# Loading x in tiles of 128 tokens instead of 116, and sending the norm factors of the dt path through DRAM

## The chip, the cores and the metric

One core of one Trainium2 chip runs the whole program. TensorE (PE) multiplies matrices and also turns them (a product with the identity); its weight loads are listed apart as PEld. VectorE (DVE), ScalarE (ACT) and GpSimd (POOL) work on tiles in on-chip memory, each through its own instructions in a fixed order; SyncE (SP) and ScalarE issue transfers, which run on 16 DMA engines. The metric is the device time of the core in microseconds, as the median of several runs: 3075.25 us before the change (3 runs, 3072.14 to 3075.53).

## The reference

A hybrid decoder trunk: 16 learned meta tokens are put ahead of 1024 tokens of width 1024, then come a Mamba-2 (SSD) mixer, a gated feed-forward layer with a short convolution, stick-breaking attention with shared keys and values, and a second feed-forward layer. The change touches only the very start:

```python
h = jnp.concatenate([meta_tokens, x], axis=1)            # 1040 tokens
u = _rmsnorm(h, ssd_norm)                                # x * rsqrt(mean(x*x) + eps) * gain
z, xbc, dt_raw = jnp.split(u @ w_in, [...], axis=-1)     # the last 32 columns are dt_raw
dt = jax.nn.softplus(dt_raw + dt_bias)
...                                                      # conv, SSD scan, gate, h + ... @ w_out
```

So the start needs x turned (features on the partitions, tokens along the row), its norm factor for each token, the normalized and turned x as the operand u of all projections, and dt_raw for the path that makes the decays of the SSD scan.

## The kernel before

**Tokens.** The 1040 tokens are cut into nine chunks of 116 (the last has 112), `CH`, and into three groups of three chunks, `TT`: 348, 348 and 344 tokens. The projections work on one group at a time, so a projection of one block of 128 output columns is three tiles. The SSD scan works on chunks of 116 and the dt path puts chunk i of group j at column `[i, j]` of a tile with 116 partitions.

**`load_x`.** Nine tiles hold x, one chunk each, tokens on the partitions; the pool has `XB` = 8 buffers, so the ninth tile waits until the first is no longer read. The loads go alternately to SyncE's and ScalarE's queue (L296 to L299). `stream(j)` takes a group: three squares with a sum over the row, on VectorE for the chunks in `SQD` (L318) and else on ScalarE (L320); then for each of eight blocks k of 128 features three transposes into a PSUM bank of the pool `lg` (two buffers, L325), a copy of it to the tile h (ScalarE for odd k, L328, VectorE for even k, L330) and a matmul that adds block k to dt_raw (L331); then the norm factors of the group from the sums (`token_rstd`, L204 to L210), written to `r9`. With the third group each finished h row is stored to DRAM (`h_d`, L333), from where the mixer's residual fetches it much later. `scaled(j)` multiplies the three x tiles in place by their factors (L342), turns them again, block by block, into PSUM banks of the pool `sm` (L347), and `parts` (L258 on ScalarE, L259 on VectorE) splits each with the gain into a high and a low part, uh and ul. `ORD` sets the order of these six pieces in the text: stream 0, scaled 0, stream 1, scaled 1, stream 2, scaled 2; products of u with the weights (`mm3`, L153 to L155, three per block) come as soon as their operands are there.

**Weights.** `load_w` fetches 128 x 1024 floats by SyncE's queue (L139) into one of three buffers, which the tile wdt of dt's weights shares; ScalarE rounds them to the high part (L146) and GpSimd subtracts (L147).

**dt path.** Its first steps turn the dt rows (L398), multiply them by the factors `r9` (L407, VectorE) and add a bias; the path is a generator, advanced between the first projections, and its result goes to DRAM (acs_d, ea_d) and back, as the decays of the scan.

**Order.** Up to the scan the instructions are ordered by the framework: each engine's list is fixed at build time, by when the framework's own model expects operands and buffers to be ready. On each engine it is then worked off strictly in order. Transfers that one queue issues wait in its order as well.

Of the kernel before, what the change touches and what calls it, by code (L numbers as in the profile page):

```python
# [20 lines left out]
CB = 116  # L21
CH = [(c * CB, min(CB, L - c * CB)) for c in range(9)]
TT = [(0, 348), (348, 348), (696, 344)]
# [24 lines left out]
SUMS = ((6, 1), (3, 6), (7, 6), (3, 5), (5, 7)), ((4, 7), (2, 1))  # L48
LPOOL = ((2, 2), (2, 4), (2, 6), (2, 7))
ORD = ((0, 0), (1, 0), (0, 1), (1, 1), (0, 2), (1, 2))  # L50
XB, SQD = 8, (1, 4, 7)
SCALE = 0.125


# [12 lines left out]
class Trunk:  # L67
# [213 lines left out]
    def load_x(self, pool, mx):  # L281

        nc, a = self.nc, self.a
        H = HEADS
        ss = self.cp.tile([P, 9], F32, tag="ss0", name="ss0")
        nc.vector.memset(ss, 1.0)
        wdt = self.wp.tile([P, 1024], F32, tag="w32", name="wdt")
        self.ln_exp()
        d = self.dp.tile([KD, P, L], F32, tag="h0_d", name="h0_d")
        r9 = mx.tile([P, 3, 3], F32, tag="r9", name="r9")  # L290
        dt = self.ex("dtr")
        xs = []
# [12 lines left out]
        u = [(self.Q("uh", F32R), self.Q("ul", F32R)) for _ in range(KD)]  # L305
        for t in (t for hl in u for t in hl):
            nc.gpsimd.tensor_copy(t[:, :HALO], self.zero)
        hs = [self.Q("h") for _ in range(KD)]

        def stream(j):  # L310
            s0, nn = TT[j]
            x3 = xs[3 * j : 3 * j + 3]
            for i in range(3):
                c = 3 * j + i
                n = CH[c][1]
                t = self.wp.tile([P, D], F32, tag="wl", name=self.nm("junk"))
                if c in SQD:
                    nc.vector.scalar_tensor_tensor(t[:n, :], x3[i][:n, :], 1.0, x3[i][:n, :], op0=ALU.mult, op1=ALU.mult, accum_out=ss[:n, c : c + 1])  # L318
                else:
                    nc.scalar.activation(t[:n, :], x3[i][:n, :], AF.Square, accum_out=ss[:n, c : c + 1])  # L320
            for k in range(KD):
                ps = self.lg("xT")
                for i in range(3):
                    n = CH[3 * j + i][1]
                    nc.tensor.transpose(ps[:, i * CB : i * CB + n], x3[i][:n, k * P : k * P + P], self.ident[:n, :n])  # L325
                h = hs[k][:, s0 : s0 + nn]
                if k % 2:
                    nc.scalar.activation(h, ps[:, :nn], AF.Copy)  # L328
                else:
                    nc.vector.tensor_copy(h, ps[:, :nn])  # L330
                nc.tensor.matmul(dt[j * H : j * H + H, :nn], wdt[:, k * H : k * H + H], h, start=k == 0, stop=k == KD - 1)  # L331
                if j == 2:
                    nc.sync.dma_start(d[k], hs[k][:, :L])  # L333
            self.token_rstd(ss[:, 3 * j : 3 * j + 3], CB, 3, y=r9[:, :, j])

        def scaled(j):
            s0, nn = TT[j]
            x3 = xs[3 * j : 3 * j + 3]
            for i, t in enumerate(x3):
                n = CH[3 * j + i][1]  # L340
                r = r9[:n, i : i + 1, j]
                nc.vector.tensor_scalar(t[:n, :], t[:n, :], r, None, op0=ALU.mult)  # L342
            for k in range(KD):
                ps = self.sm("xr")
                for i in range(3):
                    n = CH[3 * j + i][1]
                    nc.tensor.transpose(ps[:, i * CB : i * CB + n], x3[i][:n, k * P : k * P + P], self.ident[:n, :n])  # L347
                self.parts(ps[:, :nn], u[k], s0, nn, self.par("ssd_norm", k))
# [1183 lines left out]
```

## Time and profile before

| | |
|---|---|
| median of 3 runs | 3075.25 us (3072.14 to 3075.53) |
| the profiled execution, span | 3077.5 us |
| busy: PE, DVE, ACT, POOL | 94%, 76%, 53%, 46% |
| bytes read from and written to HBM | 201.25 MB, 53.45 MB |
| loads of x | 400 KB (with 64 KB of meta), seven of 464 KB, 448 KB |
| other loads at the start | params 272 KB, wdt 128 KB, heads 32 KB, weights 512 KB each |
| first dt transposes (L398) | at 102.2 us |

The profile shows one execution, 2.25 us above the median of the runs. A row of the timeline or of the chain begins with the start and the length in us; "out<-in" names the tiles by the program's names without their numbers; what stands in brackets is how long the engine had been idle before and what released it. In a row by stretches stand the stretch, its length, then for each engine its busy time with the number of instructions, and last the clock that TensorE was granted (1.00 is full), the busy share of the 16 DMA engines and the GB/s that they moved.

### The profile page before, as it was taken

Reading aid. Unit: us, or ns where it says so; the run is one execution under the profiler, and the core shown is the slowest. Engines: PE = TensorE matmul, PEld = TensorE weight load, DVE = VectorE, ACT = ScalarE, POOL = GpSimd, SP = SyncE. Lnnn points to the kernel's source line nnn. Section 1 sums busy time; section 2 is a strip of 40 time slices with the busy share of each in tenths; the row PEclk is TensorE's granted clock in tenths of the full one; section 3 lists DMA queues with packets and bytes.
Section 4 is the critical chain, followed back from the end, with each engine's and each line's share of the span. In section 5 each row is a group of like instructions: output and inputs, shape, how many; then the busy total and the mean of one; then the engine's idle time right before and its main releaser. Section 6 shows DMA issues by size and latency. Waiting matters only on the chain.

```text
span 3077.5 us, 58674 instructions
## 1 busy us (share of the span) xinstructions
PE 2897.7 (94%) x22535; PEld 2782.2 (90%) x22535; DVE 2336.0 (76%) x4030; ACT 1645.5 (53%) x3403; POOL 1411.6 (46%) x1289
## 2 busy tenths in 40 slices
PE   5999999989998999998999999999897999998997
PEld 2999898879988999998999999999797999998996
DVE  3576868885369888778966888888759888888874
ACT  2555545553245555654334888777635555554332
POOL 1154435452335666657733222222225666666741
PEclk8999999999999999999999999999998999999998
DMA  3333323323221222244132222221431222225221
GB/s 110 108 93 93 105 88 109 101 71 138 70 83 56 83 77 75 80 136 152 47 122 77 64 60 67 62 57 48 140 112 59 80 84 77 76 86 179 76 97 55
DMA packets 123220, 273.41 MB, mean 89 GB/s; under 512 B 13468, under 2 KB 53020, under 8 KB 122940
## 3 DMA queue, kind: packets, MB, share of 16 engines
q1 hardware_dynamic: 117622, 258.54, 26.9%
q10 hardware_dynamic: 4054, 6.56, 0.6%
q8 instruction: 177, 2.90, 0.4%
q0 software_dynamic: 1264, 4.57, 0.4%
q14 instruction: 103, 0.84, 0.1%
HBM read 201.25 MB, written 53.45 MB: 83 GB/s over the span
## 4 chain that ended last, share of the span: by engine, by line
PE 67%; DVE 17%; ACT 5%; issue 5%; DMA 3%; POOL 2%; ACTq 0%; POOLq 0%; SPq 0%; DVEq 0%
PE p L153 9%; PE p L154 9%; PE p L155 9%; PE acc L153 5%; PE acc L154 5%; PE acc L155 5%; PE pj L153 5%; PE pj L154 5%; PE pj L155 5%; DVE gl L992 3%; PE po L1297 2%; PE lg L1255 2%; DMA x<-in_x 1%; PE wT L1282 1%; DVE D L573 1%
## 5 line engine op out<-in xcount | busy, mean ns | idle before, releaser
L153 PE MATMUL pj<-uh,wh 128*128 128x348 f32 (+2 forms) x1536 | 507.0, 330 | 16.1 <-DVE qs L1206 7.2
L154 PE MATMUL pj<-ul,wh 128*128 128x348 f32 (+2 forms) x1536 | 497.3, 324 | 0.0
L155 PE MATMUL pj<-uh,wl 128*128 128x348 f32 (+2 forms) x1536 | 495.6, 323 | 0.0
L154 PE MATMUL p<-bl,fh 128*128 128x262 f32 x1408 | 400.9, 285 | 14.1 <-DVE bl L814 14.1
L153 PE MATMUL p<-bh,fh 128*128 128x262 f32 x1408 | 402.1, 286 | 2.5 <-ACT fh L845 1.4
L155 PE MATMUL p<-bh,fl 128*128 128x262 f32 x1408 | 400.1, 285 | 0.0
L846 POOL TENSOR_TENSOR fl<-x,fh 128x1024 fp32r<-128x1024 f32 x88 | 212.5, 2416 | 353.3 <-ACT fh L845 275.4
L147 POOL TENSOR_TENSOR wl<-w,wh 128x1024 fp32r<-128x1024 f32 (+2 forms) x80 | 163.9, 2051 | 351.8 <-ACT wh L146 351.7
L153 PEld LDWEIGHTS pj<-uh,wh 128*128 128x128 f32 x1536 | 291.8, 190 | 23.7 <-DVE qs L1206 9.2
L154 PE MATMUL p<-bl,wh 128*128 128x262 f32 x1056 | 303.1, 287 | 8.7 <-DVE bl L814 8.7
L153 PE MATMUL p<-bh,wh 128*128 128x262 f32 x1056 | 302.3, 287 | 6.2 <-ACT bh L813 6.2
L155 PE MATMUL p<-bh,wl 128*128 128x262 f32 x1056 | 301.2, 286 | 0.0
L154 PEld LDWEIGHTS pj<-ul,wh 128*128 128x128 f32 x1536 | 292.0, 190 | 1.2 <-issue 0.5
L155 PEld LDWEIGHTS pj<-uh,wl 128*128 128x128 f32 x1536 | 291.4, 190 | 0.5 <-issue 0.2
L278 DVE SCALAR_TENSOR_TENSOR c<-p,params,c 128x260 f32<-128x260 f32 x528 | 251.4, 484 | 47.2 <-ACT c L275 37.5
L153 PE MATMUL acc<-gh,wh 128*128 128x260 f32 x896 | 262.1, 293 | 22.9 <-DVE p L1037 10.7
L154 PEld LDWEIGHTS p<-bl,fh 128*128 128x128 f32 x1408 | 267.2, 190 | 16.3 <-DVE bl L814 16.0
L153 PEld LDWEIGHTS p<-bh,fh 128*128 128x128 f32 x1408 | 266.8, 190 | 5.2 <-ACT bh L813 2.0
L154 PE MATMUL acc<-gl,wh 128*128 128x260 f32 x896 | 260.3, 291 | 9.8 <-DVE gl L992 9.5
L155 PEld LDWEIGHTS p<-bh,fl 128*128 128x128 f32 x1408 | 266.6, 190 | 0.1
L886 DVE TENSOR_TENSOR c<-c,c 128x260 f32<-128x260 f32 x176 | 255.7, 1453 | 7.5 <-ACT c L882 4.5
L155 PE MATMUL acc<-gh,wl 128*128 128x260 f32 x896 | 259.0, 290 | 1.2 <-POOL wl L990 1.2
(311 smaller groups left out, 8566.7 us busy)
## 6 DMA issues: line engine op xcount, KB each, us to landing
w<-in_w_up SPq DMA_DIRECT2D x88, 512.0 KB
g<-c SPq DMA_DIRECT2D x176, 130.0 KB
w<-in_w_down SPq DMA_DIRECT2D x44, 512.0 KB
w<-in_w_in SPq DMA_DIRECT2D x40, 512.0 KB
b<-g SPq DMA_DIRECT2D x32, 520.0 KB
E<-ea_d SPq DMA_DIRECT2D x32, 464.0 KB
D<-acs_d SPq DMA_DIRECT2D x32, 420.5 KB
h<-h_d SPq DMA_DIRECT2D x16, 520.0 KB
```

The lines of the kernel that those rows point to most:

```text
L147: nc.gpsimd.tensor_tensor(wl[:, :n], w32[:, :n], wh[:, :n].bitcast(F32), op=ALU.subtract)
L153: mm(out, wh, uh, start=first, stop=False, skip_group_check=joins)
L154: mm(out, wh, ul, start=False, stop=False, skip_group_check=joins)
L155: mm(out, wl, uh, start=False, stop=last, skip_group_check=joins)
L278: nc.vector.scalar_tensor_tensor(out, ps[:, o + i : o + i + n], wcol(i), out, op0=ALU.mult, op1=ALU.add)
L573: nc.vector.tensor_scalar(dk[:, i], dk[:, i], self.cols[:n, 1, cc, h0 + i : h0 + i + 1], 0.0, op0=ALU.subtract, op1=ALU.min)
L846: tt(lo[:, :n], t, hi[:, :n].bitcast(F32), op=ALU.subtract)
L886: self.last_up = tt(g[:, :FN], g[:, :FN], v[:, :FN], op=ALU.mult)
L992: tt(gl, x, gh.bitcast(F32), op=SUB)
L1255: nc.tensor.matmul(ps[:nt, :m], part[:, c0 : c0 + nt], ks[a][:, s0 : s0 + m], start=x == 0, stop=x == 1)
L1282: nc.tensor.transpose(pt[:ns, x * CB : x * CB + nt], bt[a][:nt, x * CB : x * CB + ns], self.ident[:nt, :nt])
L1297: nc.tensor.matmul(po[64 * a : 64 * a + 64, w], v[: CH[c][1], c, 64 * a : 64 * a + 64], wt[a][: CH[c][1], c, :nt], start=x == 0, stop=x == ...
```

## The change

x is loaded in nine tiles of 128 tokens, `XC`: the first has 16 meta rows and 112 of x, the last only 16 rows. All nine have a buffer. Three tiles make a group, so the groups in which x is squared, turned, copied and split are 384, 384 and 272 tokens (`XG`). The tiles of the projections and the matmuls of dt keep the old groups of 348, 348 and 344 and the old chunks of 116. Since the factors now lie by tiles of 128 (`rx`) and the dt path wants them by chunks of 116, `rx` is written to DRAM by one transfer (128 partitions x 9 floats, each float to its own place) and read back by three (116 x 3 floats each).

```diff
-XB, SQD = 8, (1, 4, 7)
+XC = [(c * P, min(P, L - c * P)) for c in range(9)]
+XG = [(0, 3 * P), (3 * P, 3 * P), (6 * P, L - 6 * P)]
+XB, SQD = 9, (1, 4, 7)
...
+        rx = mx.tile([P, 9], F32, tag="rx", name="rx")
...
-        for c, (t0, n) in enumerate(CH):
+        for c, (t0, n) in enumerate(XC):
             xt = pool.tile([P, D], F32, tag="x", name=self.nm("x"), bufs=XB)
...
+        def turned(bank, j, k):
+            ps = bank("xT")
+            for i in range(3):
+                n = XC[3 * j + i][1]
+                nc.tensor.transpose(ps[:, i * P : i * P + n], xs[3 * j + i][:n, k * P : k * P + P], self.ident[:n, :n])
+            return ps[:, : XG[j][1]]
+
         def stream(j):
+            g0, gn = XG[j]
             s0, nn = TT[j]
...
             for k in range(KD):
-                ps = self.lg("xT")
-                for i in range(3):
-                    n = CH[3 * j + i][1]
-                    nc.tensor.transpose(ps[:, i * CB : i * CB + n], x3[i][:n, k * P : k * P + P], self.ident[:n, :n])
-                h = hs[k][:, s0 : s0 + nn]
+                ps = turned(self.lg, j, k)
+                h = hs[k][:, g0 : g0 + gn]
...
-                nc.tensor.matmul(dt[j * H : j * H + H, :nn], wdt[:, k * H : k * H + H], h, start=k == 0, stop=k == KD - 1)
+                nc.tensor.matmul(dt[j * H : j * H + H, :nn], wdt[:, k * H : k * H + H], hs[k][:, s0 : s0 + nn], start=k == 0, stop=k == KD - 1)
                 if j == 2:
                     nc.sync.dma_start(d[k], hs[k][:, :L])
-            self.token_rstd(ss[:, 3 * j : 3 * j + 3], CB, 3, y=r9[:, :, j])
+            self.token_rstd(ss[:, 3 * j : 3 * j + 3], P, 3, y=rx[:, 3 * j : 3 * j + 3])

         def scaled(j):
...
+            for c in range(3 * j, 3 * j + 3):
+                n = XC[c][1]
+                nc.vector.tensor_scalar(xs[c][:n, :], xs[c][:n, :], rx[:n, c : c + 1], None, op0=ALU.mult)
             for k in range(KD):
...
+                self.parts(turned(self.sm, j, k), u[k], *XG[j], self.par("ssd_norm", k))

         for step, j in ORD:
             (scaled if step else stream)(j)
+        rd = self.dp.tile([9, P], F32, tag="r_d", name="r_d")
+        nc.sync.dma_start(rd.rearrange("c p -> p c"), rx)
+        flat = rd.rearrange("c p -> (c p)")
+        for j in range(3):
+            nc.sync.dma_start(r9[:CB, :, j], flat[3 * CB * j : 3 * CB * (j + 1)].rearrange("(i p) -> p i", p=CB))
         return d, u, dt, r9
```

The change moves instructions, since the framework orders them anew. Three places, by the lists of the engines (line, operation, out<-in, partitions x elements; numbers tell tiles of one name apart, and x_106, x_111, x_113, ... x_125 are the nine tiles of x before, x_107, x_112, ... x_126 those of now).

ScalarE, the issue of the ninth tile of x. Before, between parts of the first group:

```order
L258 ACTIVATE uh_137<-xr_262,params 128x348
L328 ACTIVATE h_166<-xT_328 128x348
L258 ACTIVATE uh_139<-xr_268,params 128x348
L299 DMA x_125<-in_x 112x1024
L258 ACTIVATE uh_141<-xr_274,params 128x348
L320 ACTIVATE junk_397,ss_99<-x_125 112x1024
```

Now, the first instructions of ScalarE, and further down the squares of group 2:

```order
L300 DMA x_107<-in_x 112x1024
L302 DMA x_114<-in_x 128x1024
L302 DMA x_118<-in_x 128x1024
L302 DMA x_122<-in_x 128x1024
L302 DMA x_126<-in_x 16x1024
L329 ACTIVATE junk_168,ss_99<-x_107 128x1024
...
L329 ACTIVATE junk_285,ss_99<-x_120 128x1024
L334 ACTIVATE h_163<-xT_192 128x384
L207 ACTIVATE rx<-ss_99 128x3
L329 ACTIVATE junk_394,ss_99<-x_122 128x1024
L208 ACTIVATE rx<-rx 128x3
L329 ACTIVATE junk_398,ss_99<-x_126 16x1024
L334 ACTIVATE h_165<-xT_204 128x384
```

The ninth tile is issued with the others, and the squares of x_120, x_122 and x_126 (sixth, seventh and ninth tile) now stand ahead of the copy h_165 of group 0.

SyncE's queue behind the last tile of x that it loads. Before:

```order
L299 DMA x_123<-in_x 116x1024
L139 DMA w_95_518<-in_w_in 128x1024
L139 DMA w_98_524<-in_w_in 128x1024
L333 DMA h_d<-h_159 128x1040
L333 DMA h_d<-h_160 128x1040
L139 DMA w_111_655<-in_w_in 128x1024
L333 DMA h_d<-h_161 128x1040
```

Now:

```order
L302 DMA x_124<-in_x 128x1024
L141 DMA w_95_524<-in_w_in 128x1024
L141 DMA w_98_530<-in_w_in 128x1024
L141 DMA w_111_661<-in_w_in 128x1024
L352 DMA r_d<-rx 128x9x1
L141 DMA w_120_768<-in_w_in 128x1024
L355 DMA r_104<-r_d 116x3x1 x3
L141 DMA w_129_880<-in_w_in 128x1024
L339 DMA h_d<-h_161 128x1040
```

The third, fourth and fifth weight tile stand ahead of all stores of h, and the four transfers of the factors among them; behind the three loads (which wait for the store of the factors) stand one weight tile and the eight stores of h.

VectorE, where the dt path first uses the factors. Before:

```order
L259 SCALAR_TENSOR_TENSOR ul_140<-xr_502,params,uh_139 128x344
L259 SCALAR_TENSOR_TENSOR ul_142<-xr_508,params,uh_141 128x344
L407 TENSOR_TENSOR dt_637<-dt_629,r_104 116x288
L408 TENSOR_TENSOR dt_637<-dt_637,heads 116x288
L278 SCALAR_TENSOR_TENSOR xbc_661<-pj_692,params,xbc_661 128x348 x2
```

Now:

```order
L261 SCALAR_TENSOR_TENSOR ul_141<-xT_503,params,uh_140 128x272
L261 SCALAR_TENSOR_TENSOR ul_143<-xT_509,params,uh_142 128x272
L411 TENSOR_TENSOR dt_643<-dt_635,r_104 116x288
L412 TENSOR_TENSOR dt_643<-dt_643,heads 116x288
L280 SCALAR_TENSOR_TENSOR xbc_667<-pj_698,params,xbc_667 128x348 x2
```

The place is the same: right behind the last parts of group 2, ahead of the convolution taps (L278, now L280) that read a projection's bank.

More of the change, by code (lines that the diff above doesn't have):

```diff
@@ L308, in load_x @@
         hs = [self.Q("h") for _ in range(KD)]
+        def turned(bank, j, k):
[4 more added lines that the diff above has]
+            return ps[:, : XG[j][1]]
         def stream(j):
+            g0, gn = XG[j]
             s0, nn = TT[j]
-            x3 = xs[3 * j : 3 * j + 3]
-            for i in range(3):
-                c = 3 * j + i
-                n = CH[c][1]
+            for c in range(3 * j, 3 * j + 3):
+                n = XC[c][1]
@@ L316, in stream @@
                 t = self.wp.tile([P, D], F32, tag="wl", name=self.nm("junk"))
                 if c in SQD:
-                    nc.vector.scalar_tensor_tensor(t[:n, :], x3[i][:n, :], 1.0, x3[i][:n, :], op0=ALU.mult, op1=ALU.mult, accum_out=ss[:n, c : c + 1])
+                    nc.vector.scalar_tensor_tensor(t[:n, :], xs[c][:n, :], 1.0, xs[c][:n, :], op0=ALU.mult, op1=ALU.mult, accum_out=ss[:n, c : c + 1])
                 else:
-                    nc.scalar.activation(t[:n, :], x3[i][:n, :], AF.Square, accum_out=ss[:n, c : c + 1])
+                    nc.scalar.activation(t[:n, :], xs[c][:n, :], AF.Square, accum_out=ss[:n, c : c + 1])
@@ L321, in stream @@
             for k in range(KD):
-                ps = self.lg("xT")
-                for i in range(3):
-                    n = CH[3 * j + i][1]
-                    nc.tensor.transpose(ps[:, i * CB : i * CB + n], x3[i][:n, k * P : k * P + P], self.ident[:n, :n])
-                h = hs[k][:, s0 : s0 + nn]
+                ps = turned(self.lg, j, k)
+                h = hs[k][:, g0 : g0 + gn]
                 if k % 2:
-                    nc.scalar.activation(h, ps[:, :nn], AF.Copy)
+                    nc.scalar.activation(h, ps, AF.Copy)
@@ L329, in stream @@
                 else:
-                    nc.vector.tensor_copy(h, ps[:, :nn])
-                nc.tensor.matmul(dt[j * H : j * H + H, :nn], wdt[:, k * H : k * H + H], h, start=k == 0, stop=k == KD - 1)
+                    nc.vector.tensor_copy(h, ps)
+                nc.tensor.matmul(dt[j * H : j * H + H, :nn], wdt[:, k * H : k * H + H], hs[k][:, s0 : s0 + nn], start=k == 0, stop=k == KD - 1)
                 if j == 2:
                     nc.sync.dma_start(d[k], hs[k][:, :L])
-            self.token_rstd(ss[:, 3 * j : 3 * j + 3], CB, 3, y=r9[:, :, j])
+            self.token_rstd(ss[:, 3 * j : 3 * j + 3], P, 3, y=rx[:, 3 * j : 3 * j + 3])
@@ L336, in scaled @@
         def scaled(j):
[L337 to L342, printed above, removed]
-            for k in range(KD):
[L344 to L348, printed above, removed]
+            for c in range(3 * j, 3 * j + 3):
+                n = XC[c][1]
+                nc.vector.tensor_scalar(xs[c][:n, :], xs[c][:n, :], rx[:n, c : c + 1], None, op0=ALU.mult)
```

## The prediction

> **What bounds the kernel now.** I read the page first, to see what the program as a whole waits for, then the chain of waits over the first 70 us, where every line of the change lies, and then the busy times by stretch.
>
> ```profile
> span 3077.5 us, 58674 instructions
> PE 2897.7 (94%) x22535; PEld 2782.2 (90%) x22535; DVE 2336.0 (76%) x4030; ACT 1645.5 (53%) x3403; POOL 1411.6 (46%) x1289
> PE   5999999989998999998999999999897999998997
> ```
>
> TensorE is busy for 94% of the span, and of its 40 slices (77 us each) the first is by far the emptiest. Work that arrives sooner there pulls everything behind it forward, as long as TensorE stays the bound behind it. The chain of waits says what the first slice waits for (start us, us, what):
>
> ```profile
> 6.43 35.52 DMA x<-in_x
> 41.98 1.23 DVE junk L318 x2
> ...
> 44.18 6.18 DVE x L342 x3
> 50.40 0.84 PE xr L347 x3
> ...
> 54.28 0.77 PE xT L325 x3
> ...
> 55.37 1.18 PE dtr L331 x2
> ...
> 57.47 0.70 PE dtr L331 x2
> 58.17 0.45 PE xT L325 x3
> ...
> 64.05 3.43 DMA x<-in_x
> ```
>
> Up to 41.98 us it is the load of x and nothing else, then the scaling of the first three tiles (L342), then TensorE, whose dt matmuls and transposes take 1.18 and 0.77 here and 0.70 and 0.45 a little later, at half and at full clock; at 64.05 the ninth tile is fetched, which had no buffer before, and TensorE waits again. By stretch (us from:to, length, busy time and count of PE, PEld, DVE, ACT, POOL, granted clock, DMA share, GB/s):
>
> ```profile
> 6.50:42.00 35.50, 10.88 (x28) 3.63 (x28) 4.58 (x14) 7.50 (x17) 0.61 (x1) 0.77 0.35 119
> 42.00:50.40 8.40, 5.17 (x25) 2.39 (x24) 8.33 (x11) 2.81 (x4) 5.41 (x2) 0.91 0.04 17
> 50.40:64.50 14.10, 14.10 (x61) 6.79 (x61) 7.47 (x14) 4.76 (x11) 0.00 (x0) 0.79 0.01 2
> 64.50:67.50 3.00, 0.01 (x1) 0.00 (x0) 0.58 (x1) 0.48 (x1) 0.00 (x0) 0.84 0.50 153
> 67.50:102.50 35.00, 34.51 (x192) 26.23 (x193) 17.67 (x38) 20.41 (x38) 2.36 (x1) 0.92 0.51 182
> 102.50:150.00 47.50, 45.88 (x286) 45.16 (x285) 30.46 (x63) 26.65 (x39) 9.91 (x5) 1.00 0.35 89
> 72.00:76.00 4.00, 4.00 (x22) 3.09 (x21) 1.96 (x7) 1.96 (x3) 0.00 (x0) 0.83 0.98 351
> ```
>
> From 50.4 us on TensorE is the bound (14.10 of 14.10, 34.51 of 35.00, 45.88 of 47.50), but for 3.00 us at 64.5. Before that it works 16 us out of 44.
>
> **Why x is slow.** Packets, MB and share of 16 engines by queue, first from 9 to 17 us, where only 116-row tiles move, then from 64.5 to 67.5 (the 112-row tile alone):
>
> ```profile
> q10 hardware_dynamic: 104, 0.41, 12.8%
> q1 hardware_dynamic: 105, 0.41, 12.7%
> ...
> q10 hardware_dynamic: 128, 0.46, 50.1%
> ```
>
> Two queues together use 25.5% of 16 engines: four engines, without a break. A packet takes 0.255 x 16 x 8.0 us / 209 = 156 ns, or 26 GB/s per engine. The 112-row tile needed 0.501 x 16 x 3.0 / 128 = 188 ns a packet and landed 3.43 us after its issue, though its 448 KB are hardly less than the others' 464; from 72 to 76 us, where 128-row tiles of h and w move, the share is 0.98. So a row count of 116 confines a transfer to four engines, and counts of 112 and 128 do not.
>
> **The change, part by part.** *The load.* x is 1040 rows of 4 KB, 4.26 MB, and params, wdt and heads with it are 272, 128 and 32 KB. On 16 engines of 26 GB/s (412 GB/s) that is 11.4 us; at the 351 GB/s that 72 to 76 us showed it is 13.4. The start costs about 2.3 us: 3.43 less seven packets per engine of 156 ns. So x is in at 13.7 to 15.7 us; I take 14.7 for the eighth and ninth tile, 13.2 for the sixth and seventh, against 41.98 and 67.48 now.
>
> *From there to the first scaled transposes.* These rows price the steps (start us, us, engine, line, what; the last is the line's own view, with least, median and greatest ns):
>
> ```profile
> 6.50 1.06 ACT L320 ACTIVATE junk<-x 116x1024 f32<-116x1024 f32 x1 [4.42 <-DMA x<-in_x]
> 7.46 0.19 ACT L320 ACTIVATION_READ_ACCUMULATOR junk<-x 116x1 f32 x1
> 18.34 0.46 ACT L328 ACTIVATE h<-xT 128x348 f32<-128x348 f32 x1 [1.47 <-PE xT L325]
> 39.57 0.20 ACT L205 ACTIVATE r<-ss 116x3 f32<-116x3 f32 x1
> 44.09 6.26 DVE L342 TENSOR_SCALAR x<-x,r 116x1024 f32<-116x1024 f32 x3
> 44.39 5.41 POOL L147 TENSOR_TENSOR wl<-w,wh 128x1024 fp32r<-128x1024 f32 x2 [34.47 <-ACT wh L146]
> ...
> L342 DVE TENSOR_SCALAR x<-x,r x9: 747/751/2849, 44.1 to 87.2; 116x1024 f32<-116x1024 f32 x8, 112x1024 f32<-112x1024 f32 x1
> ```
>
> Today ScalarE and TensorE have long done group 0 when the eighth tile lands. In the new order ScalarE must, from 13.2 us, square the sixth tile (1.25), copy an h (0.46), take a factor (0.20), square the seventh (1.25), a factor (0.20), the ninth (1.25; 16 rows, but the same 1024 elements in each), and only then copy the h of block 5 (0.46): 18.3 us. TensorE follows with a dt matmul (0.70 in the chain) and the last transposes of group 0 (0.45): 19.5. The scaling overwrites tiles that these read, so it starts at about 19.6, and takes 6.2 as now, since GpSimd's two weight splits (5.41) fall on the same time again. It ends at 25.8 against 50.4 now: **-24.6**. If the splits miss it, three scalings of 0.75 (the median of nine) take 2.3 and it is -28.5; if x comes 1 us later and TensorE is still at half clock (0.77 and 1.18), -22.8. With x 1 us early the far end is -29.5.
>
> *The ninth tile* has a ninth buffer and comes with the rest: the idle 3.00 us go, **-3.0**.
>
> *The clock.* In 67.5:102.5 it is 0.92, so 35.0 x 0.08 = 2.8 us of TensorE's work is lost to the dip that the wait at 64.5 leaves; **-2.8**, or 0 if another stall there does the same. In 50.4:64.5 it is 0.79, 14.1 x 0.21 = 3.0 lost after the stall behind the scaling. That stall comes back, at 20 to 26 us, so I leave this at 0 (-3.0 to +3.0).
>
> [...]
>
> *VectorE* was busy 7.47 + 0.58 + 17.67 = 25.7 of the 52.1 us from 50.4 to 102.5, and nothing waited long for it. The same work now has 47 us. What can bunch is the second scaling: if GpSimd's split of the third weight meets it, it takes up to 6.2 in place of 2.3, and TensorE stands behind it. **+1.0** (0 to +4).
>
> *Widths.* 384, 384 and 272 columns sum to the same 1040: the copies, parts and transposes that grow in two groups shrink in the third. 0. From the dt transposes on, the order on TensorE, VectorE and ScalarE is the old one but for a few neighbours swapped, so there is nothing to gain or lose: 0.
>
> *The factors through DRAM.* One store of 1152 single floats, three loads of 348. The nearest packets are the 464-byte ones of acs_d and ea_d, from 129 to 131.5 us, and their user is the first row below of VectorE:
>
> ```profile
> q1 hardware_dynamic: 495, 0.20, 34.6%
> ...
> 102.82 0.46 DVE L407 TENSOR_TENSOR dt<-dt,r 116x288 f32<-116x288 f32 x1 [0.22 <-PE dt L398]
> ```
>
> 0.346 x 16 x 2.5 / 495 = 28 ns each. The third factors are ready at about 27 us, a copy and three small steps behind the scaling in VectorE's order. The store has 72 packets on each of 16 engines (2.0 us), the loads, 116 rows again, 261 on each of four (7.3), with two starts of 2.3: in at about 41. VectorE asks at 102.8 - 29.4 = 73.4. **0**: 32 us of projections and transposes hide it. Behind the loads on SP's queue stand one weight tile (block 4), which TensorE's order wants six projections after the dt transposes, and the eight stores of h: the same cover and more. A packet would have to take (73.4 - 27 - 4.6) / 0.333 = 125 ns, nearly the price of 4 KB, to be seen.
>
> [...]
>
> **Sum.** -24.6 - 3.0 - 2.8 + 1.0 = -29.4. The profiled execution goes from 3077.5 to 3048.1; the median of the runs shown is 2.25 lower, 3075.25, which gives **3046**. With all the near or all the far ends of the terms the gain is 19 to 38.
>
> **Rivals.** *The start is bound by its own engines.* With x in early, half clock and VectorE's bunches set the pace up to the projections. For: in 42.00:50.40 VectorE is busy 8.33 of 8.40, and ScalarE's squares now crowd its copies. Against: from 25.8 on the order has projections to fill with. If 25 us go at half clock, 12.5 are lost in place of 3.0, and with VectorE's +4.0 in place of +1.0 the gain is 29.4 - 9.5 - 3.0 = 16.9: 3058.
>
> *The transfer is no faster.* If four engines still carry 128 rows, only the ninth tile's wait and its clock loss go: 5.8, 3069; with a new stall there, nothing. Against it stands the 0.98 of 72 to 76 us.
>
> *The factors come late, and it is slower.* Place: VectorE at the first use of r9. Behind it in VectorE's order stand the taps that free the projections' banks, so TensorE stops too. It decides from 125 ns a packet, and eats the whole gain at (102.8 - 27 - 4.6) / 0.333 = 214 ns; at 300 ns the factors land at 131.5, 29 us after the place where they are used now: 3104. For: no packet of 4 bytes with data is in this trace. Against: 464 bytes cost 28 ns.
>
> *More gain:* splits that miss the scaling and no first clock dip, over 38 us, below 3037.
>
> **Chances.** Forecast (19 to 38 us) 0.75, bound by its own engines (6 to 19) 0.13, more gain 0.03, transfer no faster 0.05 (of which 0.02 shows a gain), late factors 0.04. The runs shown spread over 3.4 us, so 0.2%, 6 us, is about what can be told from no change. Faster 0.93, within 0.2% 0.03, slower 0.04. The range, 3037 to 3058, holds the forecast and the nearer part of the first rival.
>
> **What would show it.** Right: the eighth tile lands by 16 us with the DMA share above 0.8 from 4 to 14; the scaling of group 0 begins near 20 and ends near 26; the dt transposes stand near 73 in place of 102.4; VectorE's first use of r9 waits for no DMA; behind that the two traces run alike. Wrong: a DMA share near 0.25, a half clock that lasts beyond 35 us, VectorE waited for by TensorE for over 5 us between 26 and 60, or a wait of VectorE for r_d.

## The result

The changed kernel takes **3047.6 us** (median of 4 runs, 3044.1 to 3050.1) against 3074.7 (4 runs, 3072.1 to 3075.5): a ratio of 0.9918, 95% interval 0.9904 to 0.9932, or 27.1 us less. The forecast was 3046, with a range of 3037 to 3058.

The page of the changed kernel, the lines that answer to the first ones shown of before:

```profile
span 3045.5 us, 58682 instructions
PE 2890.8 (95%) x22535; PEld 2779.1 (91%) x22535; DVE 2336.8 (77%) x4030; ACT 1646.9 (54%) x3403; POOL 1414.2 (46%) x1289
PE   8999999989989999999999999999998999998996
```

The first slice of TensorE has gone from 5 to 8 tenths, and the rest looks as before. The chain of waits over the first 70 us (start us, us, what):

```profile
2.18 12.41 DMA x<-in_x
14.61 1.15 ACT junk L329 x2
...
22.05 2.23 DVE ss L206
...
25.13 1.41 DVE x L345 x2
26.54 2.23 DVE tb L209
```

The chain waits for x until 14.6 us instead of 42.0, and the scaling of group 0 (L345) ends at 26.5 instead of 50.4. What arrives at 14.6 is the fourth tile. Later tiles are still under way, as ScalarE's wait for the sixth shows (timeline, ScalarE):

```profile
16.34 1.06 ACT L329 ACTIVATE junk<-x 128x1024 f32<-128x1024 f32 x1 [0.48 <-DMA x<-in_x]
```

By the semaphore events of their loads in the trace, the sixth tile is in at 16.3 us, the seventh at 15.0, the eighth at 17.6 and the ninth at 15.6. By stretch (columns as before: stretch, length, PE, PEld, DVE, ACT, POOL, clock, DMA share, GB/s), the changed kernel:

```profile
6.50:14.00 7.50, 1.76 (x6) 0.89 (x6) 1.78 (x4) 2.57 (x6) 0.62 (x1) 1.00 1.02 342
14.00:20.00 6.00, 5.87 (x19) 2.02 (x18) 2.95 (x11) 4.70 (x11) 0.00 (x0) 1.00 0.84 309
26.46:75.10 48.64, 46.78 (x258) 32.04 (x258) 27.87 (x53) 25.06 (x46) 4.66 (x2) 1.00 0.42 126
```

and, for the third of these rows, the kernel before, from the end of its scaling to its dt transposes:

```profile
50.40:102.30 51.90, 48.42 (x251) 32.85 (x252) 25.52 (x53) 25.65 (x49) 2.36 (x1) 0.88 0.37 132
```

The 16 DMA engines are busy while x comes (the share adds up the times of packets and can pass 1), except from 8.6 to 9.5 us, where they move 27 GB/s: just before, most of the 2 KB packets of the load of heads begin, and they last 1.2 to 1.6 us each, where 4 KB of x take some 160 ns. The column of the clock shows 1.00 throughout, but the trace has no record of the clock before 18.1 us, and up to there the same operations take longer (timeline, TensorE):

```profile
14.62 0.90 PE L317 MATMUL xT<-ident,x 128*128 128x128 f32 x3
...
18.62 0.55 PE L317 MATMUL xT<-ident,x 128*128 128x128 f32 x3
```

A pair of dt matmuls takes 1.37 us at 15.46 and 0.77 at 19.10. From 18.1 us to the dt transposes the recorded clock is full, without a dip. In the timeline, the way of the factors (SyncE's queue, then VectorE's first use of them):

```profile
29.74 0.39 SPq L352 DMA_DIRECT2D r_d<-rx  x1
...
40.35 3.83 SPq L355 DMA_DIRECT2D r<-r_d  x3
...
75.52 0.46 DVE L411 TENSOR_TENSOR dt<-dt,r 116x288 f32<-116x288 f32 x1 [0.70 <-PE dt L402]
```

The product with the factors starts at 75.52, 27.3 us earlier than before (102.82), and waits for TensorE, not for a transfer.

**How far this shift carries.** Two places can be found in every kernel: the first dt transpose (its matmul, at 102.4 us before; its weight load begins at 102.2), and the first matmul that sums squares for the gate norm (tile ms). The latter by its line's own view (least, median and greatest ns; first and last start), before and after:

```profile
L186 PE MATMUL ms<-z,ones x4: 454/456/560, 317.0 to 328.7; 128*128 128x348 f32 x4
```

```profile
L188 PE MATMUL ms<-z,ones x4: 453/507/702, 289.6 to 301.3; 128*128 128x348 f32 x4
```

317.0 less 289.6 is 27.4: nothing was won or lost between the two places. Behind 289.6 the profiled execution needs 2755.9 us, before 2760.5. These last 4.6 us need not be an effect of the change: a second profile of the changed kernel (below; its span is 3050.7) agrees with the first to 0.1 us up to the matmul of ms and differs from it by 5.3 us behind it. So the 27.3 us at the dt transposes are the gain that the traces show, and the 32.0 us between the two spans contain chance.

### The profile page after: what moved, and what is told of

It is laid out like the page before. It is cut to its first block, busy times and chain, and to the rows that moved or that the text cites. A ratio compares the mean times of both kernels' runs of the same rounds, so it can differ in the third digit from the quotient of the medians.

```text
span 3045.5 us, 58682 instructions
## 1 busy us (share of the span) xinstructions
PE 2890.8 (95%) x22535; PEld 2779.1 (91%) x22535; DVE 2336.8 (77%) x4030; ACT 1646.9 (54%) x3403; POOL 1414.2 (46%) x1289
## 3 DMA queue, kind: packets, MB, share of 16 engines
q1 hardware_dynamic: 119942, 258.74, 27.3%
## 4 chain that ended last, share of the span: by engine, by line
PE 69%; DVE 17%; ACT 5%; issue 5%; POOL 2%; DMA 2%; SPq 0%; POOLq 0%; ACTq 0%; DVEq 0%
PE p L155 9%; PE p L156 9%; PE p L157 9%; PE acc L155 5%; PE pj L155 5%; PE acc L156 5%; PE acc L157 5%; PE pj L156 5%; PE pj L157 5%; DVE gl L996 3%; PE po L1301 2%; PE lg L1259 2%; PE wT L1286 1%; DVE kp L1272 1%; DVE bl L818 1%
## 5 line engine op out<-in xcount | busy, mean ns | idle before, releaser
L280 DVE SCALAR_TENSOR_TENSOR c<-p,params,c 128x260 f32<-128x260 f32 x528 | 251.3, 484 | 48.3 <-ACT c L277 38.5
L155 PE MATMUL acc<-gh,wh 128*128 128x260 f32 x896 | 260.5, 291 | 22.1 <-DVE p L1041 10.8
```

What stands on the lines that cost most here:

```text
L155: mm(out, wh, uh, start=first, stop=False, skip_group_check=joins)
L280: nc.vector.scalar_tensor_tensor(out, ps[:, o + i : o + i + n], wcol(i), out, op0=ALU.mult, op1=ALU.add)
```

## The experiments

One table first, since most readings go by it. "Taps" is the number of convolution taps that stand in VectorE's list between the copy of the decay rows that go to DRAM and the first scaling of D, which waits for them to come back; it became the key to two misses. The two places are starts from the traces in us; the last columns are the median and its ratio to the kernel before, measured on the same chip (median there 3073.5 for e1, e2, e3 and e5, 3077.1 for e4 with six trips, e8, e6 and e7, 3074.0 for the last four rows). The framework's order differs between kernels: by the products of the projections in the traces, e1 has done 12 more than the kernel before when its dt transposes begin, e3 15 more and e8 three fewer; at 0.16 us each (45.88 us for 286 matmuls behind the dt transposes before) that is 1.9, 2.4 and 0.5 us of work. For equal work, the stretch between the places is 214.8 us in e1, 228.4 in e3 and 215.5 in e8. At the matmul of ms all have done the same number of matmuls (1842 in every trace).

| kernel | taps | dt transposes | ms | between | median us | ratio (95%) |
|---|---|---|---|---|---|---|
| before | 8 | 102.4 | 317.0 | 214.6 | 3074.7 | 1 |
| changed | 8 | 75.1 | 289.6 | 214.5 | 3047.6 | 0.9918 |
| e1 split loads | 8 | 80.3 | 293.2 | 212.9 | 3045.2 | 0.9909 (0.9894 to 0.9923) |
| e2 slow loads | 8 | 103.0 | 317.5 | 214.5 | 3074.0 | 1.0000 (0.9991 to 1.0010) |
| e3 nine buffers | 3 | 96.7 | 322.7 | 226.0 | 3078.6 | 1.0017 (1.0007 to 1.0026) |
| e5 split, nine | 3 | 76.9 | 296.4 | 219.5 | 3056.3 | 0.9946 (0.9931 to 0.9960) |
| e4 six trips | 9 | 76.5 | 330.9 | 254.4 | 3084.5 | 1.0029 (1.0019 to 1.0040) |
| e8 split, nine, dt steps early | 8 | 76.2 | 292.2 | 216.0 | 3050.2 | 0.9917 (0.9902 to 0.9932) |
| e6 splits on VectorE | 8 | 71.5 | 285.9 | 214.4 | 3041.7 | 0.9886 (0.9872 to 0.9901) |
| e7 dt's weights later | 4 | 72.2 | 291.8 | 219.6 | 3046.8 | 0.9910 (0.9894 to 0.9927) |
| changed, again | 8 | 75.0 | 289.5 | 214.5 | 3050.1 | 0.9913 (0.9896 to 0.9930) |
| e4 two trips | 8 | 75.3 | 289.8 | 214.5 | 3049.3 | 0.9914 (0.9900 to 0.9929) |
| e9 splits and weights | 8 | 71.3 | 285.8 | 214.5 | 3044.1 | 0.9900 (0.9886 to 0.9915) |
| e10 three splits | 8 | 71.9 | 286.4 | 214.5 | 3044.7 | 0.9901 (0.9886 to 0.9915) |

**Is it the load?** e1 gives the load alone to the kernel before (the first tile, cut likewise, is left out):

```diff
...
-                (nc.sync if c % 2 else nc.scalar).dma_start(xt[:n, :], a["x"][t0 - META : t0 - META + n, :])
+                q = nc.sync if c % 2 else nc.scalar
+                for r0, r1 in ((0, 112), (112, n)):
+                    if r1 > r0:
+                        q.dma_start(xt[r0:r1, :], a["x"][t0 - META + r0 : t0 - META + r1, :])
```

> The kernel before with one thing changed: each 116-row tile of x is fetched as 112 and 4 rows, so that 112 of its rows may go over all 16 engines. Tiles, groups, eight buffers and the factors' path on TensorE stay. Theory (four engines bound the load, and the load is the gain): the eighth tile lands by about 16 us in place of 42 and the scaling of group 0 ends near 26; the ninth tile still waits for a buffer (3.0 us and the clock that it costs, up to 2.8), so 3050 to 3054 us against 3075. Rival (the buffers and the order that came with 128-row tiles are the gain): 3072 to 3076. Rival (the descriptors of a load, not its engines, bound it): as slow as before or slower, since there are twice as many loads.

Measured: 3045.2 us. Its chain of waits:

```profile
5.28 9.67 DMA x<-in_x
14.96 6.04 DMA x<-in_x
...
41.38 3.61 DMA x<-in_x
```

The first eight tiles are in at 21.0 and the ninth still has its wait, so the dt transposes come at 80.3: 22.1 us earlier than before, or 24.0 for equal work. That is what was expected of this run (21 to 25 us). The median is 5 us below what was expected; at the matmul of ms e1 is 23.8 us ahead of the kernel before, so what is more lies behind that place, where executions of one kernel differ by as much. At this place the load alone gives 23.8 of 27.4 us. By the medians e1 gains as much as the whole change (0.9909 beside 0.9918, the intervals overlap). e2 takes the load away from the changed kernel:

```diff
-                (nc.sync if c % 2 else nc.scalar).dma_start(xt[:n, :], a["x"][t0 - META : t0 - META + n, :])
+                q = nc.sync if c % 2 else nc.scalar
+                for r0, r1 in ((0, min(n, 124)), (124, n)):
+                    if r1 > r0:
+                        q.dma_start(xt[r0:r1, :], a["x"][t0 - META + r0 : t0 - META + r1, :])
```

> The changed kernel with each 128-row tile of x fetched as 124 and 4 rows, both on four engines; everything else (nine buffers, wide groups, the factors through DRAM) as changed. Theory: the DMA share goes back to 0.25, the eighth tile lands at 40 to 45 us, and of the gain only the ninth tile's wait and its clock loss are left (5.8), less the 3 to 4 us that TensorE spends more on the thin and wide tiles: 3070 to 3078 us. Rival (the gain is in the tiles, the ninth buffer or the order): 3047 to 3055.

Measured: 3074.0, ratio 1.0000. The queues from 9 to 17 us (packets, MB, share of 16 engines), and its chain:

```profile
q1 hardware_dynamic: 104, 0.43, 13.1%
q10 hardware_dynamic: 106, 0.40, 12.3%
```

```profile
29.61 16.01 DMA x<-in_x
...
47.87 6.27 DVE x L348 x3
```

The share is 25.4% again and x comes until 45.6, 3.7 us later than before, since the first eight tiles now hold 1024 rows and not 928. The scaling ends 3.8 us later than before (54.1), the stretch from there to the dt transposes is 3.0 shorter (48.9), and nothing is left of the gain: without the faster load, the 128-row tiles, the nine buffers and the trip of the factors no more than make up for its 3.7 us. The share goes with the row count in all four cases that the traces show: it is 0.255 for 116 rows and 0.254 here for 124, and 1.0 for 128 rows and, in e1, for 112. Why it does, and what other row counts give, is not shown.

**The ninth buffer.** e3 is the kernel before with one more buffer, e5 has the split loads of e1 and this edit:

```diff
-XB, SQD = 8, (1, 4, 7)
+XB, SQD = 9, (1, 4, 7)
```

> The kernel before with nine buffers for x in place of eight. Theory: only the 3.0 us wait for the ninth tile goes and the clock dip behind it (2.8): 3069 to 3072 us, the load still ends beyond 42 us. Rival (buffers and order are the gain): about 3048. If the dip of the clock stays or the wait moves elsewhere: 3073 to 3076.

> Both of the above: 116-row tiles fetched as 112 and 4 rows, and nine buffers; no 128-row tile, no wide group, no trip of the factors through DRAM. Theory (the load and the ninth tile are the whole gain, and the thin tile and the wide groups cost TensorE 3 to 4 us): 3043 to 3046 us, a little better than the changed kernel's 3047.6. If wide tiles and DRAM trip are worth something of their own: 3050 to 3055. If they cost nothing: 3047 to 3048.

Measured: 3078.6, 5 us slower than before, and 3056.3, 11 us slower than e1. Both expectations missed. e3's dt transposes do come 5.7 us earlier than before, and e5's 25.5, where its forecast asked for 29 to 32 us in all. But 11.4 and 5.0 us are lost between the dt transposes and the matmul of ms, 226.0 and 219.5 us in place of 214.6. That does not explain all of e5's time: at the matmul of ms it is 3.2 us behind e1, and why the medians are 11 apart is open. Between the two places VectorE stands still in e5 (timeline, VectorE):

```profile
103.83 0.51 DVE L446 COPY rows<-rows 96x348 f32<-96x348 f32 x1
105.66 1.81 DVE L278 SCALAR_TENSOR_TENSOR xbc<-pj,params,xbc 128x348 f32<-128x348 f32 x3 [1.33 <-ACT xbc L275]
116.54 1.61 DVE L577 TENSOR_SCALAR D<-D,cols 116x116 f32<-116x116 f32 x8 [9.06 <-DMA D<-acs_d]
```

The decay rows go to DRAM and come back as D. VectorE has three taps to do meanwhile and then waits 9.06 us; the taps behind D free the projections' banks, so TensorE stops too (timeline, TensorE):

```profile
120.00 0.40 PE L153 MATMUL pj<-uh,wh 128*128 128x348 f32 x1 [4.24 <-DVE xbc L278]
```

In e3 the same wait is 8.89 us. TensorE stands twice there, 4.59 us ahead of 108.44, where VectorE's taps come behind steps of the dt path itself, and 6.0 beside the wait for D; the clock falls to 0.83 and 0.90 (TensorE's timeline, then two stretches):

```profile
108.44 0.63 PE L153 MATMUL pj<-uh,wh 128*128 128x352 f32 x1 [4.59 <-DVE xbc L278]
```

```profile
100.00:120.00 20.00, 15.41 (x83) 15.14 (x83) 13.45 (x26) 9.93 (x15) 3.10 (x3) 0.83 0.09 26
120.00:145.00 25.00, 18.99 (x108) 18.47 (x107) 11.00 (x26) 15.56 (x20) 4.25 (x2) 0.90 0.47 128
```

The kernel before and the changed one have eight taps there. A buffer more is all that e3 changes in the text, so the new order of the lists comes from it. e8 tests whether the few taps are the cost: e5 with the steps of the dt path one projection tile earlier, which brings the taps back to eight and changes no load, buffer or work.

```diff
-                if n % 3 == 2:
+                if n % 3 == 1:
                     next(dt, None)
```

> The kernel with 112 + 4 row loads and nine buffers (3056 us), with the three steps of the dt path advanced one projection tile earlier (after tiles 1, 4 and 7 in place of 2, 5 and 8); no load, buffer or amount of work differs. VectorE's list then has eight convolution taps between the copy of the rows that go to DRAM and the first scaling of D, as the kernel before and the changed kernel have; with nine buffers and the old places it had three. Theory (nine buffers cost 11 us only because three taps do not cover the 9 us trip of acs_d through DRAM, TensorE runs out of banks and its clock dips): 3042 to 3048 us, VectorE's wait for D near 5 us, no idle TensorE above 2 us at 100 to 130. Rival (the ninth buffer itself, or the bunched start, costs it): 3054 to 3058.

Measured: 3050.2, ratio 0.9917 against 0.9946 for e5; two us above the upper end of what was expected, on a chip where the kernel before is 3.6 us slower than for e5. The wait:

```profile
103.34 0.52 DVE L446 COPY rows<-rows 96x348 f32<-96x348 f32 x1 [2.60 <-PE rows L444]
104.55 3.26 DVE L278 SCALAR_TENSOR_TENSOR xbc<-pj,params,xbc 128x344 f32<-128x344 f32 x6 [0.69 <-ACT xbc L275]
108.68 1.20 DVE L278 SCALAR_TENSOR_TENSOR xbc<-pj,params,xbc 128x348 f32<-128x348 f32 x2 [0.87 <-ACT xbc L275]
114.49 2.18 DVE L577 TENSOR_SCALAR D<-D,cols 116x116 f32<-116x116 f32 x8 [4.61 <-DMA D<-acs_d]
```

The wait is 4.61 in place of 9.06, and the stretch between the two places shrinks from 219.5 to 216.0, or 215.5 for equal work. So the explanation that the taps must cover the trip holds for e5's loss there; of e3's loss it is the second half, and the first was not tried alone. A third case came from another experiment (e7, below): four taps, 219.6.

**The factors through DRAM.** The store and its three loads, done twice and six times in a row (six are shown):

```diff
-        nc.sync.dma_start(rd.rearrange("c p -> p c"), rx)
...
-        for j in range(3):
-            nc.sync.dma_start(r9[:CB, :, j], flat[3 * CB * j : 3 * CB * (j + 1)].rearrange("(i p) -> p i", p=CB))
+        for _ in range(6):
+            nc.sync.dma_start(rd.rearrange("c p -> p c"), rx)
+            for j in range(3):
+                nc.sync.dma_start(r9[:CB, :, j], flat[3 * CB * j : 3 * CB * (j + 1)].rearrange("(i p) -> p i", p=CB))
```

> The changed kernel with the trip of the factors done twice. Theory (14.8 us a trip, 31 us of cover): the second trip ends at 58 to 62 us, 13 to 17 us before the dt path asks: no difference from the changed kernel (within 3 us), VectorE's first use of r waits for no DMA. Rival (the single floats slow the transfers of weights beside them, or the weight tile behind the trip is needed soon): 3 to 15 us slower than the changed kernel.

> The changed kernel with the trip of the factors (one store, three loads) done six times in a row on SyncE's queue; everything else as changed. One trip took 29.7 to 44.5 us in the trace of the changed kernel, 14.8 us, and the dt path asks at 75.5. Theory (a trip is hidden until it ends later than that): six trips end at 104 to 119 us, 28 to 43 us after the place where they are wanted, and the weight tiles and the stores of h behind them on the queue come as much later: 3070 to 3095 us, with VectorE waiting for r_d. Rival (the trip's time is not on any path, or the factors are not waited for): 3046 to 3050. Rival (the trip already costs some us now): the excess over the changed kernel is more than 45 us.

Measured: two trips 3049.3 beside 3050.1 for the changed kernel on the same chip, the two places 0.3 us later; six trips 3084.5, 1.0029 of before. In the latter VectorE's list and TensorE's:

```profile
119.96 0.46 DVE L412 TENSOR_TENSOR dt<-dt,r 116x288 f32<-116x288 f32 x1 [40.47 <-DMA r<-r_d]
```

```profile
121.05 0.63 PE L155 MATMUL pj<-uh,wh 128*128 128x352 f32 x1 [38.69 <-DVE xbc L280]
```

The sixth trip ends at 119.9, so one takes some 15 us (119.9 less 29.7, by six), and behind it TensorE stands for 38.7 us, as the rival of the late factors said it would. Once or twice it costs nothing, because the place that wants the factors is 31 us away.

**What the start still waits for.** In the changed kernel's timeline, VectorE and GpSimd around the first scaling:

```profile
21.90 2.35 POOL L149 TENSOR_TENSOR wl<-w,wh 128x1024 fp32r<-128x1024 f32 x1 [12.56 <-ACT wh L148]
22.05 2.23 DVE L206 TENSOR_SCALAR ss<-ss 128x3 f32<-128x3 f32 x1
...
24.46 2.08 DVE L345 TENSOR_SCALAR x<-x,rx 128x1024 f32<-128x1024 f32 x3
...
26.16 2.60 POOL L149 TENSOR_TENSOR wl<-w,wh 128x1024 fp32r<-128x1024 f32 x1 [1.90 <-ACT wh L148]
26.46 2.31 DVE L209 TENSOR_TENSOR tb<-rx 128x3 f32<-128x3 f32 x1
```

Two operations on three columns, 0.16 us elsewhere in this trace, last 2.2 and 2.3 us, each as long as the GpSimd operation that had begun just before it, and both stand on the chain. The two end with the GpSimd operations beside them, at 24.28 and 24.25 us and at 28.77 and 28.76, so they seem to wait these out. e6 moves GpSimd's first two splits to VectorE (the hand-over of `eng` inside `stream` is left out):

```diff
-        nc.gpsimd.tensor_tensor(wl[:, :n], w32[:, :n], wh[:, :n].bitcast(F32), op=ALU.subtract)
+        (eng or nc.gpsimd).tensor_tensor(wl[:, :n], w32[:, :n], wh[:, :n].bitcast(F32), op=ALU.subtract)
...
-            for n, _ in enumerate(self.stream(into(0))):
+            for n, _ in enumerate(self.stream(into(0), eng=self.nc.vector)):
```

> The changed kernel with the low parts of the first two weight blocks computed by VectorE in place of GpSimd; eight taps before D as before. In the changed kernel two tiny VectorE operations (128 x 3) lasted 2.23 and 2.31 us beside these GpSimd operations. Theory (a VectorE operation that starts beside a GpSimd one waits it out, 4.2 us in all, and the start up to the first scaling is on the path): VectorE spends 2 x about 0.8 to 1.2 us on the splits instead, 2 to 3 us gained, 3044 to 3046. Rival (it is hidden, or the splits on VectorE cost as much): 3047 to 3049.

Measured: 3041.7, ratio 0.9886. Its timeline of VectorE:

```profile
21.74 0.16 DVE L206 TENSOR_SCALAR ss<-ss 128x3 f32<-128x3 f32 x1
...
22.23 0.75 DVE L345 TENSOR_SCALAR x<-x,rx 128x1024 f32<-128x1024 f32 x1
22.89 1.22 DVE L149 TENSOR_TENSOR wl<-w,wh 128x1024 fp32r<-128x1024 f32 x1
```

The operation takes 0.16 again, a split on VectorE 1.22, the scaling begins 2.2 us earlier, and the dt transposes come at 71.5: 3.5 us earlier than in the changed kernel, half a microsecond more than the best expected. e7 issues the load of dt's weights behind two tiles of x on SyncE's queue, e9 joins this and e6, and e10 is e6 with a third split moved (first e7's edit, then e10's against e6):

```diff
-            if c == 0:
+            if c == 3:
                 nc.sync.dma_start(wdt[:, : KD * H], a["w_dt"])
...
-                    w.append(self.load_w(todo[i + 1][0], D, eng=eng if i == 0 else None))
+                    w.append(self.load_w(todo[i + 1][0], D, eng=eng if i < 2 else None))
```

> The changed kernel with the load of dt's weights issued on SyncE's queue behind two tiles of x instead of ahead of them. VectorE's list has only four taps between the copy of the rows and the first scaling of D, where the changed kernel has eight. Theory of the start alone: the second tile lands 2 to 3 us earlier, 3045 to 3048. Theory of the cover (few taps do not cover the trip of acs_d): the dt transposes come 0 to 2 us earlier, but TensorE stands idle 3 to 5 us near 105 to 115 and its clock dips after it: 3051 to 3057.

> Both single edits on the changed kernel that brought its dt transposes forward: the low parts of the first two weight blocks on VectorE (71.5 against 75.1 us) and dt's weights loaded behind two tiles of x (72.2). Here VectorE's list has eight taps before D. Theory (two separate waits on the path up to the first scaling): dt transposes at 68 to 70 us, 6 to 9 us less than the changed kernel. Rival (both edits remove the same slack, the load's end being the floor): dt transposes at 71 to 72, and no gain over the vector split alone (4 to 7 us less than the changed kernel).

> The changed kernel with the low parts of the first three weight blocks on VectorE in place of GpSimd. With two of them moved, a tiny VectorE operation (128 x 3) still lasted 2.09 us at 30.2 us beside GpSimd's third split. Theory (each such meeting is on VectorE's path to the parts of group 0): 1 to 2 us less than with two splits moved, so 5 to 9 us less than the changed kernel, dt transposes at 70 to 71. Rival (behind the first scaling TensorE has other work to fill with): same as with two moved.

> The changed kernel itself, unaltered, beside the next three on one chip: its ratio to the kernel before was 0.9918 (0.9904 to 0.9932), so 0.990 to 0.993 is expected again.

Measured: e7 3046.8. Its dt transposes come 2.9 us earlier than in the changed kernel, its stretch to ms takes 5.1 us more: few taps do cost what was said, but the earlier start makes up for much of it, and the time falls where the theory of the start alone had put it (3045 to 3048, against 3051 or more for the cover). Only the trace tells the two apart. e9 3044.1 and e10 3044.7, beside 3050.1 for the changed kernel on that chip: dt transposes at 71.3 and 71.9, no better than 71.5. So the early tile, the two splits and the third split are no separate waits; the rival said so for both. What sets the floor there, the end of the load or something else, is not shown. All three kernels with moved splits are faster than the changed one at the dt transposes by 3 to 4 us; by their ratios, 0.9886 to 0.9901 against 0.9913 and 0.9918, the intervals overlap, but for e6's and the first of the changed kernel, which were measured on different chips.

## Why the prediction was right, and where not

**The load: the sum right, three of its steps not.** Forecast -24.6, measured -23.8 (the scaling ends at 26.54 instead of 50.36). The sixth tile was in at 16.3 us and the eighth at 17.6, where 13.2 and 14.7 were forecast, and the scaling began at 24.46 instead of 19.6. In e6, where the small operation ahead of it takes 0.16 us, it begins at 22.23: so 2.2 us of the delay are that operation beside GpSimd's first split, and 2.6 us came earlier, in the load and the steps up to there. The scaling was shorter (2.08 for 6.2), since the splits did not meet it, as the step said, but the small operations ahead of it and behind it. That one split is waited out either way is half of why the sum came out; that the late tiles used up the rest is luck.

**The ninth tile: right, -3.0.** It lands at 15.6 us and nothing waits for it. e3 was to show this term alone and does not: its 5.7 us at the dt transposes meet the 5.8 that were forecast, but its eighth tile comes 2 us later (44.0), its scaling takes 2.07 us and not 6.26, both dips of the clock are gone, and it has done 15 products more by then. That a buffer more could cost 5 to 11 us further on was not in the prediction. In the changed kernel eight taps stand there as before, so it did not come about; on the sentence that behind the dt transposes the order is the old one hung more than the prediction said.

**The clock: mechanism right, size off.** Forecast -2.8, with the dip behind the scaling left in place (0, at most -3.0). Both dips went: 0.88 over 51.9 us before, 6.2 us, and 1.00 after. The stall that was to bring the first one back was the scaling of 6.2 us, and that took 2.08. In e3, where it took 2.07, there is no dip either (1.00 from 40 to 96.7 us). In e5, where the splits do meet the scaling, the dip is there (timeline and stretch):

```profile
25.95 6.23 DVE L346 TENSOR_SCALAR x<-x,r 116x1024 f32<-116x1024 f32 x3 [0.37 <-PE xT L329]
```

```profile
30.00:40.00 10.00, 8.28 (x38) 4.50 (x39) 6.17 (x13) 3.71 (x7) 1.35 (x2) 0.83 0.25 96
```

A half clock that lasts through the denser start, as the first rival has it, is not in the trace behind 18.1 us: the recorded clock is full from there to the dt transposes, with 144 transposes among the 302 matmuls up to these. Why operations take longer ahead of 18.1 us (three transposes 0.90 us, then 0.55) is not shown.

**Widths: the step that failed.** "The copies, parts and transposes that grow in two groups shrink in the third. 0." From the end of the scaling to the dt transposes TensorE was busy 48.42 us before, of which 6.2 went to the clock: 42.2 at full clock. Now it is busy 46.78, 4.6 more. 258 matmuls in place of 251 are 1.3 of it (at 0.18 each); some 3 us are left. The views of TensorE's transposes by shape, of the changed kernel in this stretch and of e3 up to its dt transposes (count | busy us, mean ns):

```profile
L317 PE MATMUL xT<-ident,x 128*128 128x128 f32 x98 | 16.9, 283 | 0.2 <-DVE ul L261 0.2
...
L317 PE MATMUL xT<-ident,x 16*128 16x16 f32 x16 | 3.4, 228 | 0.0
```

```profile
L347 PE MATMUL xr<-ident,x 116*128 116x116 f32 x64 | 10.3, 265 | 0.0
...
L325 PE MATMUL xT<-ident,x 112*128 112x112 f32 x8 | 2.1, 262 | 0.0
```

A transpose of 16 rows takes 228 ns where one of 112 takes 262. These operations overlap, so their lengths are not yet their cost. Nearer to it is the time from the start of one to the start of the next matmul, or to its own end if that is earlier (ends are modelled). Taken so from the traces at full clock, 113 transposes of the changed kernel in this stretch average 124 ns, 111 of e3 (48.3 to 96.7 us) 96 and 102 of e5 (35.6 to 76.9 us) 90, while dt matmuls average 346, 347 and 345 and products 196, 188 and 197. 28 to 34 ns on 113 transposes are 3.2 to 3.8 us, which is what was left. By shape, a transpose of 128 rows takes 120 ns and one of 116 rows 95 to 102, and the third of a triple takes 149 ns with 16 rows and 60 with 112: the columns sum to the same 1040, but the ninth tile costs more than a whole one did.

**VectorE +1.0:** the row of stretches has TensorE idle for 1.86 us, 1.6 less than before, where 3.0 went with the ninth tile. So there are new waits of 1.4 us, near the forecast, but they come with the second of the small operations and not with the second scaling.

**The sum.** -23.8, then -1.6 of idle time, -6.2 of clock, +4.6 of work: -27.0, which is the shift seen at the dt transposes but for 0.3 of rounding at the edges; -29.4 was forecast. The sum must close, since the 4.6 is what the other terms leave; the transposes and the seven matmuls, taken by themselves, give 4.5 to 5.1. The clock gave 3.4 more and the widths took 4.6. That these two nearly cancel is luck, and the median of 3047.6 lies near the forecast also for that reason.

**The factors: 0, right.** Forecast in at 41 us; by the semaphore events of the three loads the last was in at 46.5, with 29 us to spare. The size inside was off: the store and the wait for it took 10.6 us (29.74 to 40.35), 4.3 were forecast.

**Rivals and signs.** A start bound by its own engines did not happen: the clock is full from 18.1 us and the new waits are 1.4 us. A transfer that is no faster is what e2 made, and it gave 3074. Late factors are what six trips made. Of the signs that were named for being right, the eighth tile by 16 us (17.6) and a scaling that begins near 20 (24.5) did not show; its end near 26, the dt transposes (75.1 for 73), VectorE's use of the factors without a wait and the like traces behind them did.

## What to carry to other kernels

Look at a load's row count before its bytes: 116 rows kept 4 of 16 DMA engines at work (a share of 0.255, where 128 rows gave 1.0), and the whole first slice waited for it. A last tile of 16 rows cost TensorE no less here than one of 112 (149 ns a transpose beside 60). When a schedule is made by a model, compare the lists far behind the edit as well, at every place where an engine waits for a round trip: one more buffer, which removed a wait of 3 us, moved five taps away from such a place, and with the split loads that cost some 4 us there. A start that reproduces to 0.1 us shows a gain of 3 us that the medians of 3000 us do not.

## What the runs showed of the hardware that was not expected

**Rows and the price of a packet.** From 10 to 14 us, the changed kernel (128-row transfers) and e1 (112-row ones and 4-row ones between them):

```profile
DMA packets 489, 1.67 MB, mean 418 GB/s; under 512 B 81, under 2 KB 81, under 8 KB 489
...
q1 hardware_dynamic: 250, 0.89, 56.2%
q10 hardware_dynamic: 228, 0.78, 48.3%
```

```profile
DMA packets 298, 1.04 MB, mean 259 GB/s; under 512 B 45, under 2 KB 45, under 8 KB 298
...
q1 hardware_dynamic: 158, 0.55, 54.9%
q10 hardware_dynamic: 140, 0.49, 46.2%
```

The share is 1.0 in both, but a packet of 4 KB takes 1.045 x 16 x 4.0 us / 408 = 164 ns in the one and 1.011 x 16 x 4.0 / 253 = 256 ns in the other (packets under 512 B left out), and the eighth tile of x is in at 21.0 in e1 and at 17.6 in the changed kernel. With 128 rows a packet costs as little on sixteen engines as 116-row ones did on four (156). Whether the 112 rows or the 4-row transfers among them cause it was not tried.

**Small operations beside GpSimd.** What such an operation loses does not grow with its own size here: 128 x 3 elements waited for 2.1 us, and so did a scaling of 116 x 1024 in the kernel before (2849 ns at most, with a median of 751).
